# A transformer block with PEER: 160 tokens by gathers instead of 128, spread to the last steps, and their outputs made inside the main loop

## The chip, the cores and the metric

The kernel runs on one core of a Trainium2 chip. The metric is the time of one execution on the device, in microseconds (us). Engines: PE (TensorE, matmuls), DVE (VectorE), ACT (ScalarE), POOL (GpSimd), SP (SyncE, which here only issues DMAs).

## What is computed

One encoder layer for 512 tokens of width 1024: adaLN modulation, multi-head latent attention beside a gated MLP, a projection, and then PEER, 16,384 experts of a single neuron each. The part that the change touches is PEER and the final norm:

```python
def peer(h, w_q, keys, U, V):
    q = (ht @ w_q).reshape(T, 8, 2, 128)
    s1 = einsum('thd,hkd->thk', q[:, :, 0], keys[:, 0])     # 128 keys each
    s2 = einsum('thd,hkd->thk', q[:, :, 1], keys[:, 1])
    v1, i1 = top_k(s1, 16); v2, i2 = top_k(s2, 16)
    sc, ci = top_k(v1[..., :, None] + v2[..., None, :], 16) # of 256 sums
    idx = i1[ci // 16] * 128 + i2[ci % 16]                  # 8 x 16 experts a token
    gates = softmax(sc)
    a = einsum('chkd,cd->chk', U[idx], x)
    return einsum('chkd,chk->cd', V[idx], gelu(a) * gates)
x = x + gate2 * peer(h2);  out = rmsnorm(x) * g_final
```

So each token needs 128 rows of `U` and of `V` (16384 x 1024, float32).

## The kernel before

The 512 tokens are treated in two ways. `TD` = 384 tokens (blocks 0 to 2 of 128) are **dense**: all 16,384 experts are computed for them, 128 at a time, as matmuls, and a gate table `gd`, zero for experts that a token did not choose, picks out the right ones. Block 3 (`GB`) is **gathered**: for each of its tokens' 128 choices, an indirect DMA on POOL fetches 128 rows of `peer_u` (`gu`, `gather_u`, L871) and later of `peer_v` (`gv`, `gather_v`, L881), 512 KB at a time into one of four buffers (tag `g`); DVE multiplies a `gu` tile by the tokens and sums (L875), and adds a `gv` tile, weighted, to `accg` (L887).

Below, an expert e is a block of 128 neurons. Every float32 product is made of three matmuls of parts that PE takes (`mm3`, L80: high x high, high x low, low x high), so each operand is split first (`split_into`, L76: ACT copies the high part, DVE subtracts for the low part, `...h` and `...l`). For each expert, `a_mm` (L509) makes `pa`, 8 x 3 matmuls with the transposed tokens `h2T` moving (`TD` columns); ACT's gelu gives `a`; DVE multiplies `a` by the gate table (L938) and splits it into `w...h`, `w...l`; v is loaded and split (L935); then 3 token blocks x 2 halves x 3 = 18 matmuls add to the six accumulators `out0` to `out5` (512 columns each).

In time: 0 to 256 us, everything ahead of PEER; 256 to 455, queries, scores and routing of the dense blocks, with the first products of 20 experts between; 455 to 594, the gate table, in `NG = TD // UT` groups of eight tokens (`g_eq`, `g_gate`, `g_mm` L788, `g_evac`), with ten experts between; then the main loop of 128 steps. Step e makes `pa` of expert e + 30 (`AHEAD`; in steps 0 to 97) and `out` of expert e. The last four experts (`TAIL`, 124 to 127) are held and multiplied together at the end. After the loop each block's output is made: half by half a product with `gate2` out of `out...` (L979), an add of the residual `xr` (L980), ACT's squares, a root on POOL, the gain `gfin` (L985, L997) and two stores.

What goes between the steps is set by a planner: `fill` is a list of pieces of work with a cost, first the routing of block 3, then its 128 `gather_u`, then 128 `gather_v`. Each step has a `slack` (4.6 in steps with `pa`, 1.7 without, 0 in the last `END` = 8), and pieces are issued as the running sum of slack times `rate` (all costs over all slack) passes their costs. The pieces follow v's split in DVE's order. SP issues the loads of u, v, the gate table and `xr`, and half the stores, in the order of its queue.

Of the kernel before, what the change touches and what calls it, by code (L numbers as in the profile page):

```python
# [19 lines left out]
P = 128  # L20
# [9 lines left out]
TD = ND * P  # L30
# [6 lines left out]
END = 8  # L37
# [20 lines left out]
def tile_kernel(ctx: ExitStack, tc: tile.TileContext, a: dict, out: bass.AP):  # L58
# [442 lines left out]
    gtg = pp.tile([P, 1, PH, K], F32, name="gtg")  # L501
    jrep = pp.tile([P, K, K], BF16, name="jrep")
# [98 lines left out]
    def route_lookup(r, f, dst):  # L601
# [6 lines left out]
        nc.vector.tensor_tensor(oh, oh, r["rep"].pop(f), op=ALU.mult)  # L608
# [17 lines left out]
    with ExitStack() as qs:  # L626
# [8 lines left out]
        for b in range(NB):  # L635
            nc.vector.tensor_scalar_mul(xn[b], x2[b], r2[b])
        for j in range(KD):
            p = q_ps(f"trx2{j}")
            for b in range(ND):
                nc.tensor.transpose(p[:, b * P:(b + 1) * P], xn[b][:, j * P:(j + 1) * P], ident)  # L640
            t = W.tile([P, TD], F32, name=f"nt2_{j}", tag="qT", bufs=3)
            affine(j, t, p[:, :TD], s2, sh2)
            split_into(h2T[0][:, j, :TD], h2T[1][:, j, :TD], t)
# [9 lines left out]
        split_into(h2T[0][:, :, TD:], h2T[1][:, :, TD:], tg)  # L653
# [6 lines left out]
        nc.scalar.dma_start(h2gd, h2gt)  # L660
# [20 lines left out]
        def score(h):  # L681
            s_sb = R.tile([P, ND, 2, P], F32, name=f"s{h}", tag="s_sb", bufs=3)
            s_gb = R.tile([P, 2, P], F32, name=f"sg{h}", tag="s_gb", bufs=2)
            for f in range(2):
# [14 lines left out]
                nc.scalar.copy(s_sb[:, :, f, :], p[:, :TD].rearrange("p (b n) -> p b n", n=P))  # L699
                nc.scalar.copy(s_gb[:, f, :], p[:, TD:])  # L700
# [40 lines left out]
    flat = lambda t, b: t.rearrange("p b h k -> p b (h k)")[:, b, :]  # L741
    vp = pool(ctx, "vpool")
# [102 lines left out]
    def gb_open():  # L845
        st["stack"] = ExitStack()
        st["R"] = pool(st["stack"], "gbroute")
        st["sg"] = st["R"].tile([P, 2 * PH, P], F32, name="sgb")
        nc.sync.dma_start(st["sg"], sgd)
        st["r"] = route_tiles(st["R"], "g", 1, PH)  # L850
        st["sc"] = st["R"].tile([P, 1, PH, K], F32, name="scg")
        st["i"] = [st["R"].tile([P, 1, PH, K], F32, name=f"i{f}g") for f in range(2)]

    def gb_idx():
# [3 lines left out]
        st["gp"] = pool(ctx, "gpool")  # L858
        st["accg"] = st["gp"].tile([P, D], F32, name="accg")
        st["h2g"] = st["gp"].tile([P, D], F32, name="h2g")  # L860
        nc.sync.dma_start(st["h2g"], h2gd)
        st["actg"] = st["gp"].tile([P, NS], F32, name="actg")
        st["wg"] = st["gp"].tile([P, NS], F32, name="wg")

    def gather(src, s, name):
        g = st["gp"].tile([P, D], F32, name=name, tag="g", bufs=4)
        nc.gpsimd.indirect_dma_start(out=g, out_offset=None, in_=src,  # L867
                                     in_offset=bass.IndirectOffsetOnAxis(ap=idx[:, s:s + 1], axis=0))
        return g

    def gather_u(n):  # L871
        g = gather(a["peer_u"], n, f"gu{n}")
        actg, wg = st["actg"], st["wg"]
        scr = st["gp"].tile([P, D], BF16, name=f"scr{n}", tag="scr", bufs=1)
        nc.vector.scalar_tensor_tensor(scr, g, 1.0, st["h2g"], op0=ALU.mult, op1=ALU.mult,  # L875
                                       accum_out=actg[:, n:n + 1])
        if n == NS - 1:
            nc.scalar.activation(wg, actg, AF.Gelu)
# [10 lines left out]
    fill = []  # L889
    for h in range(PH):  # L890
        for f in range(2):
            fill.append((1.6, lambda h=h, f=f: route_keys(st["r"], 0, h, f, st["sg"][:, 2 * h + f, :])))
    fill.append((0.0, lambda: (route_tables(st["r"]), route_rep(st["r"], 0))))
    fill.append((1.2, lambda: route_cands(st["r"])))
    for h in range(PH):
        fill.append((1.3, lambda h=h: route_pick(st["r"], 0, h, st["sc"][:, 0, h, :])))
    fill.append((3.6, lambda: route_decode(st["r"])))
    fill.append((4.0, lambda: route_lookup(st["r"], 0, st["i"][0])))
    fill.append((0.0, lambda: route_rep(st["r"], 1)))
    fill.append((4.0, lambda: route_lookup(st["r"], 1, st["i"][1])))  # L900
    fill.append((1.2, lambda: route_gates(st["R"], st["sc"], gtg, PH)))
    fill.append((0.3, gb_idx))
# [10 lines left out]
    due = 0.0  # L913
    gb_open()
    for e in range(NE):
# [27 lines left out]
        if e < NE - TAIL or e == NE - 1:  # L943
            for b in range(ND):
                bs = slice(b * P, (b + 1) * P)
                for hf, (e_, wh, wl, vh, vl) in [(hf, h) for hf in range(2) for h in held]:
                    sl = slice(hf * 512, (hf + 1) * 512)
                    mm3(outs[2 * b + hf], (wh[:, bs], wl[:, bs]), (vh[:, sl], vl[:, sl]),
# [132 lines left out]
```

## Time and profile before

| | us |
|---|---|
| median of three runs | 1552.92 (1550.22 to 1554.04) |
| the profiled execution | 1551.62 |
| its span in the trace | 1549.8 |
| PE busy | 1485.2 (96%) |
| DVE busy | 1234.8 (80%) |
| ACT busy | 649.1 (42%) |
| POOL busy | 393.5 (25%) |
| DMA traffic | 380.72 MB, mean 246 GB/s |

The shares are over the whole span, and stages differ, so the rows below go stage by stage. Matmuls overlap each other: the printed duration of one is longer than the time from its start to the next one's, and only the pitch of starts says what one costs. A tile's number is its expert's or its gather's; where a view groups instructions, the number is left out.

### The profile page before, as it was taken

The numbers are of one execution on the slowest core, as the hardware profiler recorded it, in microseconds if no ns is written. First come the engines' busy times: TensorE is split into PE (matmuls) and PEld (weight loads), VectorE is DVE, ScalarE is ACT, GpSimd is POOL, SyncE is SP. The second block draws the span as 40 slices with busy tenths as digits, with TensorE's granted clock in tenths as the row PEclk, the third lists the DMA queues.
The fourth block names the chain that finished last, engine by engine and source line by source line (L and its number), as shares of the span: only waits on it lengthen the run. The fifth ranks groups of instructions, "written<-read, shape, count | busy, mean of one in ns | idle before, by whom it ended". The sixth has DMA issues, their size and how long they took to land.

```text
span 1549.8 us, 21464 instructions
## 1 busy us (share of the span) xinstructions
PE 1485.2 (96%) x7675; PEld 1311.7 (85%) x7675; DVE 1234.8 (80%) x2385; ACT 649.1 (42%) x1097; POOL 393.5 (25%) x335
## 2 busy tenths in 40 slices
PE   2898999999989999999999999999999999999997
PEld 1665687888979999999999999999999999998885
DVE  6937865569999997988878788788888788887774
ACT  2543434434459995443333333333333333333342
POOL 1212100000000000004444454444444444443210
PEclk9999999999989999999999999999999999999999
DMA  9626444331426778768999899898998899887872
GB/s 365 228 91 221 126 143 147 115 106 49 130 81 199 224 237 261 242 210 314 328 321 332 327 325 327 314 316 325 334 330 317 311 328 327 321 315 239 257 245 95
DMA packets 147228, 380.72 MB, mean 246 GB/s; under 512 B 11185, under 2 KB 59841, under 8 KB 146865
## 3 DMA queue, kind: packets, MB, share of 16 engines
q1 hardware_dynamic: 102896, 219.97, 40.6%
q0 software_dynamic: 42352, 153.62, 28.9%
q10 hardware_dynamic: 1872, 5.77, 1.0%
q8 instruction: 60, 0.98, 0.2%
q14 instruction: 48, 0.39, 0.1%
HBM read 349.16 MB, written 30.15 MB: 245 GB/s over the span
## 4 chain that ended last, share of the span: by engine, by line
PE 85%; DVE 8%; DMA 3%; issue 2%; ACT 1%; POOL 0%; SPq 0%; POOLq 0%; DVEq 0%; ACTq 0%
PE out L84 11%; PE out L83 11%; PE out L82 11%; PE pa L84 11%; PE pa L83 11%; PE pa L82 11%; PE gg L792 6%; DMA wada<-w_ada 2%; PE q L82 1%; PE q L83 1%; PE q L84 1%; DVE macc L149 1%; PE yo L83 1%; PE yo L84 1%; PE yo L82 1%
## 5 line engine op out<-in xcount | busy, mean ns | idle before, releaser
L867 POOL DMA_INDIRECT gu<-peer_u,idx x128 | 178.0, 1391 | 641.2 <-PE out L83 443.3
L867 POOL DMA_INDIRECT gv<-peer_v,idx x128 | 173.5, 1356 | 236.8 <-DVE accg L887 205.9
L887 DVE SCALAR_TENSOR_TENSOR accg<-gv,wg,accg 128x1024 f32<-128x1024 f32 x127 | 162.9, 1282 | 10.7 <-DMA gv<-peer_v,idx 8.5
L875 DVE SCALAR_TENSOR_TENSOR scr<-gu,h2g 128x1024 bf16<-128x1024 f32 x128 | 156.5, 1223 | 15.3 <-DMA gu<-peer_u,idx 12.9
L792 PE MATMUL gg<-o,o 128*128 128x128 f32 x768 | 96.1, 280 | 1.6 <-ACT o L786 1.6
L792 PEld LDWEIGHTS gg<-o,o 128*128 128x128 f32 x768 | 95.1, 196 | 1.9 <-ACT o L786 1.9
L938 DVE TENSOR_TENSOR a<-a,g 128x384 f32<-128x384 f32 x128 | 69.2, 551 | 4.7 <-ACT g L803 2.4
L786 ACT ACTIVATE o<-o1b,gT 128x128 f32<-128x128 bf16 x192 | 63.4, 404 | 13.2 <-PE gg L792 8.0
L518 ACT ACTIVATE a<-pa 128x384 f32<-128x384 f32 x128 | 61.5, 482 | 3.2 <-PE pa L84 3.1
L149 DVE SCALAR_TENSOR_TENSOR macc<-wada,csil,macc 128x1024 f32<-128x1024 f32 x40 | 51.3, 1282 | 10.5 <-DMA wada<-w_ada 10.1
L775 DVE TENSOR_TENSOR o<-iota_s,gT 128x1024 f32<-128x1024 f32 x48 | 58.7, 1222 | 0.6 <-PE gg L792 0.5
L779 DVE TENSOR_SCALAR o<-iota_s,gT 128x128 f32<-128x128 f32 x192 | 53.5, 345 | 0.0
L801 ACT COPY st<-gg 128x512 f32<-128x512 f32 x96 | 50.3, 578 | 0.0
L159 PE MATMUL mcol<-ident_s,macc 128*128 128x128 f32 x32 | 7.4, 390 | 26.7 <-DVE macc L146 22.8
L135 POOL DMA_DIRECT2D wada<-w_ada x32 | 17.1, 535 | 60.7 <-DVE macc L149 25.5
L159 PEld LDWEIGHTS mcol<-ident_s,macc 128*128 128x128 f32 x32 | 5.5, 201 | 28.5 <-DVE macc L146 18.3
L424 ACT ACTIVATE pe<-s,mx 128x512 f32<-128x512 f32 x16 | 11.0, 689 | 29.4 <-DVE mx L422 21.2
L773 DVE TENSOR_TENSOR o1b<-erep,gB 128x512 bf16<-128x512 bf16 x48 | 20.2, 422 | 1.1 <-ACT gB L756 1.1
L697 PE MATMUL sc<-keys_s,qT 128*128 128x128 f32 x128 | 18.0, 284 | 0.9 <-ACT qT L694 0.9
L697 PEld LDWEIGHTS sc<-keys_s,qT 128*128 128x128 f32 x128 | 15.5, 191 | 3.6 <-ACT qT L694 2.2
L531 DVE MAX8 v12d<-s 128x8 f32<-128x128 f32 x48 | 12.8, 285 | 6.9 <-ACT s L699 6.9
L418 PE MATMUL s<-kr,qr 64*128 64x512 f32 x32 | 18.0, 641 | 0.0
(2792 smaller groups left out, 4941.0 us busy)
## 6 DMA issues: line engine op xcount, KB each, us to landing
gd<-st SPq DMA_DIRECT2D x12, 1984.0 KB, 7.9
g<-gd SPq DMA_DIRECT2D x31, 768.0 KB, 8.5
wada<-w_ada POOLq DMA_DIRECT2D x32, 512.0 KB, 4.8
wada<-w_ada SPq DMA_DIRECT2D x16, 512.0 KB, 10.1
x<-x SPq DMA_DIRECT2D x4, 512.0 KB, 12.4
x<-x ACTq DMA_DIRECT2D x4, 512.0 KB, 4.1
x2d<-x ACTq DMA_DIRECT2D x4, 512.0 KB, 2.8
gu<-peer_u,idx POOLq DMA_INDIRECT x128, 7.0
```

Of the source, the lines that this page charges most:

```text
L82: nc.tensor.matmul(o, lhsT=lh, rhs=rh, start=first, stop=False)
L83: nc.tensor.matmul(o, lhsT=lh, rhs=rl, start=False, stop=False)
L84: nc.tensor.matmul(o, lhsT=ll, rhs=rh, start=False, stop=last)
L149: nc.vector.scalar_tensor_tensor(acc, w, csil[:, c:c + 1], acc, op0=ALU.mult, op1=ALU.add)
L518: nc.scalar.activation(t, p[:, :TD], AF.Gelu)
L775: nc.vector.tensor_tensor(o2s[n], iota.unsqueeze(1).to_broadcast([P, UT, P]), tT[:, 1, t0:t0 + UT].unsqueeze(2).to_broadcast([P, UT, P]), ...
L786: nc.scalar.activation(o1s[n][:, i, :], e[:, :, i], AF.Copy, scale=tT[:, 2, t0 + i:t0 + i + 1])
L792: nc.tensor.matmul(pgs[n][i // 4][:, i % 4 * P:(i % 4 + 1) * P], lhsT=o2[:, i, :], rhs=o1[:, i, :], start=True, stop=True)
L867: nc.gpsimd.indirect_dma_start(out=g, out_offset=None, in_=src, in_offset=bass.IndirectOffsetOnAxis(ap=idx[:, s:s + 1], axis=0))
L875: nc.vector.scalar_tensor_tensor(scr, g, 1.0, st["h2g"], op0=ALU.mult, op1=ALU.mult, accum_out=actg[:, n:n + 1])
L887: nc.vector.scalar_tensor_tensor(accg, g, wg[:, s:s + 1], accg, op0=ALU.mult, op1=ALU.add)
L938: nc.vector.tensor_tensor(wv3, wv3, gt[:, :, e % GE, :], op=ALU.mult)
```

## The change

Of the 384 dense tokens the last 32 (`XT`) are moved to gathers, so `TD` becomes 352 while the routing still covers `TR` = 384. For these 32 tokens the 128 choices are laid out as four quarters (`XQ`) of 32 choices (`XS`) over the 128 partitions: 32 `gather_u` and 32 `gather_v` more, with sums per quarter in `accx`, which a matmul with a 0/1 matrix `xsel` adds up (`px`, two halves). Their expert numbers and gates go through small DRAM tables (`xid`, `xgd`), their tokens through `h2gd`. The gate table has 44 groups instead of 48. `pa` is 352 columns wide. The third token block has 96 rows.

The planner's list becomes: one `gather_u` of the x tokens after each piece of routing, the rest of the routing, x's `gather_v`, block 3's gathers, and then the outputs of the x tokens and of block 3 as two pieces of cost 4.0. `END` is 3 instead of 8, and a late step's slack 2.0 instead of 1.7. The score tables of block 3 are loaded head by head, the copy `route_rep` is dropped in its lookups (the multiplication reads a broadcast), and the gathers' pool is opened at the loop's start. Cut to its core:

```diff
-TD = ND * P
+TR = ND * P
+XT = 32
+TD = TR - XT
+XQ = P // XT
+XS = NS // XQ
-END = 8
+END = 3
...
+        tx = XN.tile([P, KD, XT], F32, name="tx")
         for j in range(KD):
...
-            split_into(h2T[0][:, j, :TD], h2T[1][:, j, :TD], t)
+            split_into(h2T[0][:, j, :TR], h2T[1][:, j, :TR], t)
+            nc.vector.tensor_copy(tx[:, j, :], t[:, TD:])
...
+        h2xt = XN.tile([XT, D], F32, name="h2xt")
+        for i in range(2):
+            p = q_ps(f"h2xp{i}")
+            for j in range(4):
+                nc.tensor.transpose(p[:XT, j * P:(j + 1) * P], tx[:, 4 * i + j, :], ident)
+            nc.scalar.copy(h2xt[:, i * 512:(i + 1) * 512], p[:XT])
+        nc.scalar.dma_start(h2gd[P:], h2xt)
...
+    nc.vector.scalar_tensor_tensor(xi[xr_], flat(i1a, ND - 1)[xr_], 128.0, flat(i2a, ND - 1)[xr_],
+                                   op0=ALU.mult, op1=ALU.add)
+    nc.sync.dma_start(xid.rearrange("q t s -> t q s"), xi[xr_].rearrange("t (q s) -> t q s", q=XQ))
+    nc.sync.dma_start(xgd.rearrange("q t s -> t q s"), flat(gts, ND - 1)[xr_].rearrange("t (q s) -> t q s", q=XQ))
+    nc.sync.dma_start(idxx, xid.rearrange("q t s -> (q t) s"))
+    nc.sync.dma_start(gtx, xgd.rearrange("q t s -> (q t) s"))
...
+    def g_open(k, ns):
+        h2g = gp.tile([P, D], F32, name=f"h2g{k}", tag="h2g", bufs=1)
...
+        if b == "x":
+            p = psa.tile([P, 512], F32, name=f"px{hf}", tag="pa", bufs=2)
+            nc.tensor.matmul(p[:XT], lhsT=st["xsel"], rhs=gs_["x"]["acc"][:, halves[hf]], start=True, stop=True)
+            return p
...
+    for n in range(XS):
+        fill.append((1.3, lambda n=n: gather_u("x", idxx, gtx, n, XS)))
+        if n < len(route):
+            fill.append(route[n])
+    fill += route[XS:]
+    for n in range(XS):
+        fill.append((1.3, lambda n=n: gather_v("x", idxx, n)))
     for n in range(NS):
-        fill.append((1.3, lambda n=n: gather_u(n)))
+        fill.append((1.3, lambda n=n: gather_u("g", idx, flat(gtg, 0), n, NS)))
     for n in range(NS):
-        fill.append((1.3, lambda n=n: gather_v(n)))
-    slack = [4.6 if e + AHEAD < NE else 1.7 for e in range(NE)]
+        fill.append((1.3, lambda n=n: gather_v("g", idx, n)))
+    fill.append((0.3, out_open))
+    for b in ("x", GB):
+        fill.append((4.0, lambda b=b: output(b)))
+    slack = [4.6 if e + AHEAD < NE else 2.0 for e in range(NE)]
...
-                bs = slice(b * P, (b + 1) * P)
+                bs = slice(b * P, min((b + 1) * P, TD))
...
-    for b in (GB, 0, 1, 2):
+    for b in range(ND):
         o_load(b)
-        if b == GB:
-            o_sum(b, 0)
-            o_gain(b)
-            o_sum(b, 1)
-            o_root(b)
-            o_store(b)
```

What moves in the engines' orders, at three places. First DVE in the middle of the main loop, from one split of `w` to the next (`v...l` and `u...l` are splits, `accg` the sum over a gathered tile, `a` the gate product). Before:

```order
L78 TENSOR_TENSOR w74l_10964<-a74_8782,w74h_10963 128x384
L935 TENSOR_TENSOR v72l_10820<-v72r_10817,v72h_10819 128x1024
L887 SCALAR_TENSOR_TENSOR accg_6540<-gv33_10846,wg_6544,accg_6540 128x1024
L887 SCALAR_TENSOR_TENSOR accg_6540<-gv34_10849,wg_6544,accg_6540 128x1024
L887 SCALAR_TENSOR_TENSOR accg_6540<-gv35_10852,wg_6544,accg_6540 128x1024
L78 TENSOR_TENSOR u103l_10858<-u103r_10855,u103h_10857 128x1024
L938 TENSOR_TENSOR a101_10742<-a101_10742,g100_12688 128x384
L78 TENSOR_TENSOR w75l_11035<-a75_8858,w75h_11034 128x384
```

With the change:

```order
L82 TENSOR_TENSOR w78l_11361<-a78_9100,w78h_11360 128x352
L1063 TENSOR_TENSOR v76l_11211<-v76r_11208,v76h_11210 128x1024
L938 SCALAR_TENSOR_TENSOR accg_10737<-gvg21_11237,wgg_7844,accg_10737 128x1024
L938 SCALAR_TENSOR_TENSOR accg_10737<-gvg22_11240,wgg_7844,accg_10737 128x1024
L82 TENSOR_TENSOR u107l_11252<-u107r_11249,u107h_11251 128x1024
L938 SCALAR_TENSOR_TENSOR accg_10737<-gvg23_11243,wgg_7844,accg_10737 128x1024
L1066 TENSOR_TENSOR a105_11133<-a105_11133,g104_12971 128x352
L938 SCALAR_TENSOR_TENSOR accg_10737<-gvg24_11246,wgg_7844,accg_10737 128x1024
L82 TENSOR_TENSOR w79l_11432<-a79_9176,w79h_11431 128x352
```

Here four gathered tiles stand in a step instead of three, and the operations on `a` and `w` are 352 wide.

Second, DVE at the end of the loop, where the last experts' splits and the first output work stand. Before (`yf0` is the first product of block 0's output):

```order
L78 TENSOR_TENSOR w125l_13480<-a125_12443,w125h_13479 128x384
L935 TENSOR_TENSOR v123l_13433<-v123r_13430,v123h_13432 128x1024
L78 TENSOR_TENSOR w126l_13491<-a126_12511,w126h_13490 128x384
L935 TENSOR_TENSOR v124l_13464<-v124r_13461,v124h_13463 128x1024
L78 TENSOR_TENSOR w127l_13502<-a127_12584,w127h_13501 128x384
L935 TENSOR_TENSOR v125l_13475<-v125r_13472,v125h_13474 128x1024
L979 TENSOR_TENSOR yf0_13602<-out0_5451,gate2_84 128x512
```

With the change, from the x tokens' first product on (`yfx`, `ygx`, `ssfx`: the x tokens' output; `yf3`, `yg3`, `ssf3`: block 3's):

```order
L977 TENSOR_TENSOR yfx_13613<-px0_13616,gate2_84 32x512
L1063 TENSOR_TENSOR v124l_13670<-v124r_13667,v124h_13669 128x1024
L978 TENSOR_TENSOR yfx_13613<-yfx_13613,xrx_13611 32x512
L977 TENSOR_TENSOR yfx_13613<-px1_13622,gate2_84 32x512
L983 TENSOR_TENSOR ygx_13615<-yfx_13613,gfin_13549 32x512
L978 TENSOR_TENSOR yfx_13613<-yfx_13613,xrx_13611 32x512
L987 TENSOR_TENSOR ssfx_13614<-ssfx_13614 32x1
```

and right behind these rows:

```order
L977 TENSOR_TENSOR yf3_13680<-accg_10737,gate2_84 128x512
L118 TENSOR_SCALAR finx_ms_13628<-ssfx_13614 32x1
L977 TENSOR_TENSOR yf3_13680<-accg_10737,gate2_84 128x512
L994 SCALAR_TENSOR_TENSOR yfx_13613<-yfx_13613,finx_r_13630,gfin_13549 32x512
L978 TENSOR_TENSOR yf3_13680<-yf3_13680,xr3_13678 128x512 x2
L983 TENSOR_TENSOR yg3_13682<-yf3_13680,gfin_13549 128x512
L1063 TENSOR_TENSOR v125l_13702<-v125r_13699,v125h_13701 128x1024
L987 TENSOR_TENSOR ssf3_13681<-ssf3_13681 128x1
L82 TENSOR_TENSOR w127l_13729<-a127_12728,w127h_13728 128x352
L118 TENSOR_SCALAR fin3_ms_13691<-ssf3_13681 128x1
L994 SCALAR_TENSOR_TENSOR yf3_13680<-yf3_13680,fin3_r_13693,gfin_13549 128x512
L977 TENSOR_TENSOR yf0_13806<-out0_5381,gate2_84 128x512
```

The outputs of the x tokens and of block 3 now stand ahead of `v125l` and `w127l`; before, block 3's were done ahead of `w125l`. On PE the two matmuls of `px` stand ahead of the first one of expert 123.

Third, SP's queue at the end. Before:

```order
L971 DMA xr3_13579<-x2d_87 128x1024
L927 DMA v121r_13372<-peer_v 128x1024
L971 DMA xr0_13600<-x2d_87 128x1024
L927 DMA v122r_13401<-peer_v 128x1024
L927 DMA v123r_13430<-peer_v 128x1024
L1000 DMA out_0_dram<-yf3_13581 128x512
```

With the change:

```order
L1055 DMA v124r_13667<-peer_v 128x1024
L966 DMA xr1_13809<-x2d_87 128x1024
L966 DMA xr3_13678<-x2d_87 128x1024
L966 DMA xr2_13814<-x2d_87 96x1024
L997 DMA out_0_dram<-yfx_13613 32x512
L966 DMA xr0_13804<-x2d_87 128x1024
L997 DMA out_0_dram<-yf3_13680 128x512
```

Block 0's residual `xr0` was loaded before v122; now it comes after all expert loads and behind a store of the x tokens' output.

## Rows read from the trace of the kernel before

**Rows 1.** The page, chain that ended last, share by engine.
```profile
PE 85%; DVE 8%; DMA 3%; issue 2%; ACT 1%; POOL 0%; SPq 0%; POOLq 0%; DVEq 0%; ACTq 0%
```
**Rows 2.** Stretches: from:to, us, busy us (and instructions) per engine, PE clock, DMA share, GB/s.
```profile
345.00:452.00 107.00, 101.18 (x534) 90.72 (x532) 105.34 (x495) 47.88 (x64) 0.00 (x0) 1.00 0.32 104
455.00:594.00 139.00, 138.46 (x1053) 138.49 (x1054) 133.79 (x299) 125.40 (x323) 0.00 (x0) 0.98 0.67 205
594.00:720.00 126.00, 126.00 (x635) 114.81 (x634) 106.90 (x325) 52.60 (x71) 9.46 (x7) 1.00 0.72 246
1010.00:1300.00 290.00, 290.00 (x1456) 263.89 (x1455) 235.82 (x262) 101.05 (x141) 136.41 (x97) 1.00 0.90 323
```
**Rows 3.** Timeline of PE in the loop: start, us, instruction.
```profile
1189.69 0.34 PE L83 MATMUL pa<-h2T,u101h 128*128 128x384 f32 x1
...
1193.05 0.34 PE L84 MATMUL pa<-h2T,u101l 128*128 128x384 f32 x1
1193.23 0.39 PE L82 MATMUL out<-v71h,w71h 128*128 128x512 f32 x1
...
1197.12 0.40 PE L84 MATMUL out<-v71h,w71l 128*128 128x512 f32 x1
```
**Rows 4.** Timeline of DVE in the loop, with idle time before and what ended it.
```profile
1181.12 0.56 DVE L78 TENSOR_TENSOR w73l<-a,w73h 128x384 fp32r<-128x384 f32 x1 [0.75 <-ACT w73h L77]
1182.08 1.23 DVE L935 TENSOR_TENSOR v71l<-v71r,v71h 128x1024 fp32r<-128x1024 f32 x1 [0.40 <-ACT v71h L934]
1183.22 3.92 DVE L887 SCALAR_TENSOR_TENSOR accg<-gv,wg,accg 128x1024 f32<-128x1024 f32 x3
...
1189.50 0.56 DVE L78 TENSOR_TENSOR w74l<-a,w74h 128x384 fp32r<-128x384 f32 x1 [0.75 <-ACT w74h L77]
```
**Rows 5.** Chain in order of time: start, us, what; groups of the gate table.
```profile
463.14 1.78 PE gg L792 x16
...
590.93 1.78 PE gg L792 x16
```
**Rows 6.** The page, groups: busy us, mean ns | idle before, what ended it.
```profile
L887 DVE SCALAR_TENSOR_TENSOR accg<-gv,wg,accg 128x1024 f32<-128x1024 f32 x127 | 162.9, 1282 | 10.7 <-DMA gv<-peer_v,idx 8.5
L875 DVE SCALAR_TENSOR_TENSOR scr<-gu,h2g 128x1024 bf16<-128x1024 f32 x128 | 156.5, 1223 | 15.3 <-DMA gu<-peer_u,idx 12.9
```
**Rows 7.** Timeline of POOL in the same loop step.
```profile
1184.77 1.86 POOL L867 DMA_INDIRECT gv<-peer_v,idx  x1 [3.59 <-DVE accg L887]
```
**Rows 8.** The tile `gv`: time from issue to landing.
```profile
DMA to landing us min/median/max: 4.4/6.6/10.7
```
**Rows 9.** Timeline of DVE in steps without `pa`.
```profile
1419.66 0.56 DVE L78 TENSOR_TENSOR w102l<-a,w102h 128x384 fp32r<-128x384 f32 x1 [0.71 <-ACT w102h L77]
...
1423.74 0.56 DVE L78 TENSOR_TENSOR w103l<-a,w103h 128x384 fp32r<-128x384 f32 x1 [0.71 <-ACT w103h L77]
```
**Rows 10.** Timelines of PE (first row) and DVE at the end.
```profile
1517.06 0.39 PE L82 MATMUL out<-v123h,w123h 128*128 128x512 f32 x1
...
1526.17 0.69 DVE L979 TENSOR_TENSOR yf<-out,gate 128x512 f32<-128x512 f32 x1 [2.34 <-PE out L84]
...
1530.44 0.16 DVE L991 TENSOR_TENSOR ssf<-ssf 128x1 f32<-128x1 f32 x1 [0.79 <-ACT xr L981]
...
1541.63 0.75 DVE L997 SCALAR_TENSOR_TENSOR yf<-yf,fin_r,gfin 128x512 f32<-128x512 f32 x1 [0.72 <-POOL fin_r L114]
```
**Rows 11.** Chain in order of time: float32 matmuls of 512 columns.
```profile
81.83 1.72 PE qn L342 x4
```
**Rows 12.** DMA issues at the end: count, KB each, median us from issue to landing.
```profile
xr<-x2d SPq DMA_DIRECT2D x4, 512.0 KB, 4.0
out_dram<-yf SPq DMA_DIRECT2D x4, 256.0 KB, 2.3
```
**Rows 13.** DMA rate in slices of 5 us, from 1100 to 1300 us.
```profile
GB/s 273 348 297 339 412 336 313 202 366 269 413 368 343 256 252 310 310 412 398 271 341 301 216 350 330 346 321 296 358 228 388 377 347 305 358 203 314 380 388 301
```
**Rows 14.** The page, groups: the gate table's weight loads.
```profile
L792 PEld LDWEIGHTS gg<-o,o 128*128 128x128 f32 x768 | 95.1, 196 | 1.9 <-ACT o L786 1.9
```

More of the change, by code (lines that the diff above doesn't have):

```diff
@@ L857, in gb_idx, with gather @@
         st["stack"].close()
[L858 to L866, printed above, removed]
+        st["gp2"] = pool(ctx, "gpool2")
+    def gather(src, ix, s, name):
+        g = gp.tile([P, D], F32, name=name, tag="g", bufs=4)
@@ new lines, in g_open, with gather_u @@
+    def g_open(k, ns):
+        h2g = gp.tile([P, D], F32, name=f"h2g{k}", tag="h2g", bufs=1)
+        if k == "x":
+            for q in range(XQ):
+                nc.sync.dma_start(h2g[q * XT:(q + 1) * XT, :], h2gd[P:])
+        else:
+            nc.sync.dma_start(h2g, h2gd[:P])
+        gs_[k] = {"h2g": h2g,
+                  "act": gp.tile([P, ns], F32, name=f"act{k}"),
+                  "w": gp.tile([P, ns], F32, name=f"wg{k}")}
+    def gather_u(k, ix, gt_, n, ns):
+        if n == 0:
+            g_open(k, ns)
+        g = gather(a["peer_u"], ix, n, f"gu{k}{n}")
+        actg, wg = gs_[k]["act"], gs_[k]["w"]
+        scr = gp.tile([P, D], BF16, name=f"scr{k}{n}", tag="scr", bufs=1)
+        nc.vector.scalar_tensor_tensor(scr, g, 1.0, gs_[k]["h2g"], op0=ALU.mult, op1=ALU.mult,
@@ L887, in gather_v, with out_open @@
             nc.vector.scalar_tensor_tensor(accg, g, wg[:, s:s + 1], accg, op0=ALU.mult, op1=ALU.add)
-    fill = []
+    rows = {GB: (TR, T), "x": (TD, TR), 0: (0, P), 1: (P, 2 * P), 2: (2 * P, TD)}
+    halves = [slice(hf * 512, (hf + 1) * 512) for hf in range(2)]
+    outp, rs = {}, {}
+    def out_open():
+        st["gfin"] = gp.tile([P, D], F32, name="gfin", tag="g", bufs=4)
+        nc.sync.dma_start(st["gfin"], a["g_final"].partition_broadcast(P))
+        st["xsel"] = gp.tile([P, XT], F32, name="xsel")
+        nc.vector.reduce_sum(st["xsel"], ident.rearrange("p (q t) -> p t q", q=XQ), axis=AX.X)
@@ new lines, in o_store, with output @@
+    def o_store(b):
+        xr, y, ss, yg, n = outp[b]
+        r, (r0, r1) = rs[b][:, 0:1], rows[b]
+        nc.scalar.activation(yg, yg, AF.Copy, scale=r)
+        nc.vector.scalar_tensor_tensor(y[:, halves[1]], y[:, halves[1]], r, st["gfin"][:n, halves[1]],
+                                       op0=ALU.mult, op1=ALU.mult)
+        nc.scalar.dma_start(out[r0:r1, halves[0]], yg)
+        nc.sync.dma_start(out[r0:r1, halves[1]], y[:, halves[1]])
+    def output(b):
+        o_load(b)
+        o_sum(b, 0)
+        o_gain(b)
+        o_sum(b, 1)
+        o_root(b)
+        o_store(b)
@@ L897, in tile_kernel @@
[L897 to L902, printed above, removed]
+        route.append((1.3, lambda h=h: route_pick(st["r"], 0, h, st["sc"][:, 0, h, :])))
+    route.append((3.6, lambda: route_decode(st["r"])))
@@ L903, in tile_kernel @@
+    for f in range(2):
+        route.append((5.0, lambda f=f: route_lookup(st["r"], f, st["i"][f])))
+    route.append((1.2, lambda: route_gates(st["R"], st["sc"], gtg, PH)))
+    route.append((0.3, gb_idx))
+    fill = []
+    for n in range(XS):
[5 more added lines that the diff above has]
+        fill.append((1.3, lambda n=n: gather_v("x", idxx, n)))
     for n in range(NS):
-        fill.append((1.3, lambda n=n: gather_u(n)))
+        fill.append((1.3, lambda n=n: gather_u("g", idx, flat(gtg, 0), n, NS)))
@@ L913, in tile_kernel @@
     due = 0.0
+    gp = pool(ctx, "gpool")
     gb_open()
```

138 lines of the change are left out of this document (73 added, 65 removed).

## The prediction

> **What bounds the kernel now.** I read the chain of waits first: TensorE (PE) holds 85% of it, DVE 8% [rows 1]. Then busy time by stretch [rows 2]: in the main loop PE is busy 290.00 of 290.00 us with DVE at 235.82, so there a step lasts as long as its matmuls. Before the loop it differs: from 345 to 452 us DVE is busy 105.34 of 107.00, and from 455 to 594 us PE, DVE and ACT are all near full. The row to watch is the loop's: the change takes work from PE and gives DVE more, so I price both per step and see which is longer.
>
> PE's price comes from the pitch of starts, since the printed durations overlap. Twenty `pa` products of 384 columns start from 1189.69 to 1193.05: 3.36 / 19 = 0.177 us. Eighteen `out` products of 512 columns start from 1193.23 to 1197.12: 3.89 / 17 = 0.229 us [rows 3]. So 128 columns are worth 0.052 us, and 32 are worth 0.013. DVE's mid-loop step runs from the start of `w73l` to that of `w74l`: 1189.50 − 1181.12 = 8.38 us [rows 4], and 24 × 0.177 + 18 × 0.229 = 8.37 agrees.
>
> The sum below is made against the profiled execution's 1551.62 us (span 1549.8), 1.3 below the median of 1552.92. About 0.3%, 4.7 us, is what a measurement of this kernel can tell from no change.
>
> **The change part by part.**
>
> *Front, to 455 us.* Twenty experts' first products lose 480 × 0.013 = 6.2 us on PE, but DVE is the full engine there and its split of each expert is as wide as before. Added for it are eight small copies (each below the 0.56 us of an operation on 384 columns [rows 4]), then transposes and two copies on ACT. I take −1 and +1: 0, with ends −5 and +2. The four small DMAs added to SP stand between two expert loads that are fetched ahead; I cost them at nothing, and within the +2 if that cover is gone.
>
> *Gate table, 455 to 594.* A group of eight tokens recurs every (590.93 − 463.14) / 45 = 2.84 us [rows 5]. The table falls from 384 tokens to 352, 48 groups to 44, and PE, DVE and ACT all lose the same four: 48 × 2.84 = 136.3 becomes about 125.4. **−10.9**. The ten experts done between the groups are now spread over 44, which could leave DVE last: ends −8 and −11.4.
>
> *Loop, PE.* Only `pa` gets narrower: 24 × 0.013 = 0.31 us per step. The third output block has 96 rows instead of 128 but still streams 512 columns, so `out` keeps its price. A PE-bound step is 8.38 − 0.31 = 8.07.
>
> *Loop, DVE.* The planner's table gives the gathers per step. Before: 383.1 units of fill over 488.2 of slack, times 4.6 is 3.61 units or 2.78 gathers a step. After: 476.6 over 504.8, 4.34 units or 3.34 gathers a step, from about step 22 to step 97. Per step the other DVE work is v's split, u's split, the gate product and w's split: 1.23 each for the first two (one of them stands in the rows), about 0.56 each for the other two [rows 4]; less what overlaps it is 3.25, as the loop's total gives it (235.82 us over 290 / 8.38 = 34.6 steps is 6.81; less 2.78 × 1.28). At 352 columns it is 3.16. With 3.34 accumulations at 1.282 us or products at 1.223 us [rows 6] a step asks 7.44 or 7.24 us of DVE. Against 8.07 this leaves 0.63 to 0.83, so DVE still is not the longest by busy time, and what counts is how long it stands waiting for a gather.
>
> *Loop, waits for gathers.* Four buffers serve the gathers. POOL issues the next when DVE frees one: an accumulation of the three that start at 1183.22 ends near 1184.50, and POOL's gather starts at 1184.77 [rows 4, 7], 0.27 later. Landing takes 6.6 us in the median, 4.4 to 10.7 at the ends [rows 8], and use 1.28. That is 8.2 us of a buffer's cycle. Before, 97 gathers in 290 us [rows 2] grant 4 × 290 / 97 = 11.96 us: 3.8 to spare. After, 4 × 8.07 / 3.34 = 9.66: 1.5 to spare. Before, DVE waited 10.7 + 15.3 us over the 255 [rows 6], 0.10 each. With the spare cut to two fifths I take 0.24 each, an estimate in the same proportion, 0.80 a step, about the whole slack; lumps of it then reach PE. I take a step of 8.21 (ends 8.07, nothing reaching PE, and 8.6, where waits double again). 76 steps × (8.21 − 8.38) = **−12.9**; ends −23.6 and +17.
>
> *Steps 0 to 21.* Here the routing of the gathered block is filled in, and one x-gather with each piece. DVE was busy 106.90 of 126.00 [rows 2], 7.1 us a step; 0.73 more units add 0.6: 7.7 of 8.07. 22 × 0.31 is −6.9; the nearly full DVE and the first gathers (behind a load and a freed pool) give back an estimated 2: **−4.9**, ends −6.9 and +3.
>
> *Steps 98 to 123.* Only `out` remains, pitch 1423.74 − 1419.66 = 4.08 [rows 9], and the planner gives 1.46 gathers a step (1.03 before). DVE's step: 0.5 + 1.2 + 1.46 × 1.28 + 0.4 of waits for ACT = 4.0. Just fits: **+1**, ends 0 and +6.
>
> *End.* Two outputs, 32 rows and 128 rows, now sit in the last steps, behind which DVE has `v125l` and `w127l`, on which PE's last products wait. Count from T0, the start of step 123 on PE (1517.06 before); the first output's multiply of block 0 followed 9.1 us later [rows 10]. After: PE first runs the two selecting products, 4 records × 0.43 = 1.72 us [rows 11]. DVE takes the first at T0 + 0.9, then eleven half-width operations × 0.69, one split of 1.23, and waits as in the rows of before, 0.79 for ACT's squares and 0.72 for POOL's root [rows 10]: `v125l` ends near T0 + 12.7. PE, having run what it can (18 + 24 products × 0.229 + 1.72 = T0 + 11.3), stands 1.5 us. Block 0 is then whole at about T0 + 14.6 and its multiply starts at T0 + 15.1: **+6**, ends +2 and +9. On SP the load of block 0's `xr0` stands behind the store of the 32 rows, whose buffer it takes: multiplied at about T0 + 8.7, landed 2.3 later, and 4.0 for the load [rows 12] make T0 + 15.0, just ahead of its add at 15.8; if that store is late, the load is what is late next, and it sets the upper end. DVE's last run of output work (1526.17 to the product at 1541.63) starts 6 later and is as long as before; what the gathered block's output took here before was already under the loop's last matmuls.
>
> *Sum.* −10.9 + 0 − 4.9 − 12.9 + 1 + 6 = −21.7; 1551.6 − 21.7 = **1530 us**.
>
> **The rivals.**
>
> *All cover holds* (chance 0.09). No gather wait reaches PE and the end loses little: −11 + 0 − 7 − 24 and +3 to +7 for the last steps and the end is −39 to −35: 1513 to 1517. For it: DVE's busy time does fit. Against it: little spare is left in the four buffers.
>
> *The transfers' rate becomes the bound* (0.17). A step moves two expert blocks of 128 × 1024 × 4 bytes = 0.524 MB, 0.180 of gate table (128 × 352 × 4 bytes) and 3.34 gathers of 0.524: 2.98 MB. The loop ran 323 GB/s at a DMA share of 0.90 [rows 2], so 359 at full share: 8.30 us per step, 76 × −0.08 = −6, and 1537. Against it: single slices of 5 us reached 412 and 413 GB/s [rows 13]. The Trainium skill, page "DMA: Bandwidth & Descriptors", section "Where 436 GB/s comes from", says that between HBM and SBUF the HBM side binds, at about 358 GB/s for a core; by that figure a step would take 8.32 us and the kernel about 1538, and those slices of this trace speak against it as a hard limit for a core that is alone.
>
> *The four buffers' round trip becomes the bound* (0.14; the slower one). If the denser gathers land later, a step becomes 3.34 × (0.27 + L + 1.28) / 4, whatever PE needs. The rest of the sum is −8.8, so it stops being a gain at a step of 8.50, a mean landing of 8.6 us; at L = 9 the step is 8.81 and the kernel 1551.6 − 8.8 + 33 = 1576. For it: single landings of 10.7, and a DMA share that would go from 0.90 to near 1. Against it: the median of 6.6 at that 0.90.
>
> *Narrower products are no cheaper* (0.05). If loading the 128 × 128 weights set the pitch, 352 columns would take as long as 384. The weight load's record is 196 ns [rows 14], longer than the 0.177 of the pitch. Against it: sixteen such loads with 128 columns take 1.78 us, 0.111 each [rows 5], so a load of 196 ns overlaps its neighbours. Then the loop gains nothing and the table only the four groups' own products, 4 × 1.78 = 7: 1551.6 − 7 + 1 + 6, about 1552.
>
> **How the numbers follow.** The forecast has 0.55, spread from about 1522 to 1542. The range leaves out most of the buffers' rival above 1554 and half of the best case below 1514: 1514 to 1554. Faster by over 0.3%: nearly all of the forecast (0.52), the best case (0.09) and most of the rate's rival (0.14): 0.75. Within: some of each, and narrower products that are no cheaper: 0.12. Slower: mainly the buffers' rival, 0.13.
>
> **What would show it.** Gate table about 125 us long; `pa` pitch 0.164; steps 22 to 97 at 8.1 to 8.3 with some PE idle on `w…l` or `u…l` and more DVE idle on gathers; last steps still 4.1; about 15 us from T0 to block 0's multiply. The forecast is wrong if steps stay at 8.38 or above (landing beyond 8 us), if `pa` keeps 0.177, or if the end costs over 10 us.

## The result and the profile after

The changed kernel takes 1541.93 us (median of four runs, 1539.0 to 1542.88) where the kernel before took 1552.12 in the same comparison: a ratio of 0.9934, interval 0.992 to 0.9947. That is 10.2 us faster. The direction was right and the time lies in the range, but the gain is less than half of the 22 us that were forecast. The profiled execution took 1542.68 us, span 1540.8.

The page of the changed kernel, busy time and the chain that ended last, against [rows 1]:

```profile
PE 1452.5 (94%) x7623; PEld 1240.4 (81%) x7623; DVE 1279.7 (83%) x2476; ACT 638.9 (41%) x1078; POOL 455.7 (30%) x400
...
PE 41%; DMA 24%; DVE 16%; issue 10%; ACT 4%; POOL 4%; SPq 0%; POOLq 0%; DVEq 0%; ACTq 0%
DMA gug<-peer_u,idx 10%; DMA gvg<-peer_v,idx 8%; PE out L86 4%; PE out L87 4%; PE out L88 4%; PE pa L88 3%; PE pa L87 3%; PE pa L86 3%; POOL gvg L901 2%; DMA wada<-w_ada 2%; PE gg L822 2%; ACT o L816 2%; POOL gug L901 2%; PE q L87 1%; PE q L88 1%
```

PE's share of the chain fell from 85% to 41%, and the landings of gathers, which did not show among its lines before, hold 18%. The loop's stretch and the gathers' groups, against [rows 2] and [rows 6]:

```profile
1010.00:1300.00 290.00, 283.85 (x1474) 246.96 (x1474) 252.99 (x321) 103.51 (x143) 149.38 (x117) 1.00 0.97 362
```

```profile
L924 DVE SCALAR_TENSOR_TENSOR scrg<-gug,h2gg 128x1024 bf16<-128x1024 f32 x128 | 156.4, 1222 | 45.7 <-DMA gug<-peer_u,idx 44.6
L938 DVE SCALAR_TENSOR_TENSOR accg<-gvg,wgg,accg 128x1024 f32<-128x1024 f32 x127 | 163.0, 1284 | 28.8 <-DMA gvg<-peer_v,idx 27.6
```

PE no longer fills the loop: 6 us of 290 are idle. DVE's wait for the gathers of block 3 grew from 26.0 to 74.5 us. The landing of a `gv` tile, against [rows 8], rose from 6.6 to 7.4 us in the median:

```profile
DMA to landing us min/median/max: 4.9/7.4/10.1
```

By stretch, from the starts of the first instructions named (timelines of both kernels), in us:

| stretch | before | after | difference | forecast |
|---|---|---|---|---|
| start to first gate product `gg` | 455.5 | 461.2 | +5.7 | 0 |
| first to last `gg` product | 136.9 | 127.8 | −9.1 | −10.9 |
| to the first `out` of expert 22 | 190.5 | 187.3 | −3.2 | −4.9 |
| to `out` of expert 98 | 632.1 | 620.3 | −11.8 | −12.9 |
| to `out` of expert 122 | 97.9 | 105.9 | **+8.0** | +1 |
| to block 0's first multiply | 13.2 | 18.1 | +4.9 | +6 |
| to the end of the span | 23.6 | 20.2 | −3.4 | 0 |

The differences add up to −8.9, which is what separates the two profiled executions. Two lines carry the miss: the front and the steps without first products. The large loop term came out near its forecast; whether for the reason given is what the experiments ask first.

### The profile page after: what moved, and what is told of

Its sections match the earlier page's. It is cut to its first block, busy times and chain, and to the rows that moved or that the text cites. A ratio compares the mean times of both kernels' runs of the same rounds, so it can differ in the third digit from the quotient of the medians.

```text
span 1540.8 us, 21600 instructions
## 1 busy us (share of the span) xinstructions
PE 1452.5 (94%) x7623; PEld 1240.4 (81%) x7623; DVE 1279.7 (83%) x2476; ACT 638.9 (41%) x1078; POOL 455.7 (30%) x400
## 4 chain that ended last, share of the span: by engine, by line
PE 41%; DMA 24%; DVE 16%; issue 10%; ACT 4%; POOL 4%; SPq 0%; POOLq 0%; DVEq 0%; ACTq 0%
DMA gug<-peer_u,idx 10%; DMA gvg<-peer_v,idx 8%; PE out L86 4%; PE out L87 4%; PE out L88 4%; PE pa L88 3%; PE pa L87 3%; PE pa L86 3%; POOL gvg L901 2%; DMA wada<-w_ada 2%; PE gg L822 2%; ACT o L816 2%; POOL gug L901 2%; PE q L87 1%; PE q L88 1%
## 5 line engine op out<-in xcount | busy, mean ns | idle before, releaser
L901 POOL DMA_INDIRECT gug<-peer_u,idx x128 | 169.8, 1327 | 147.5 <-DVE scrg L924 123.2
L901 POOL DMA_INDIRECT gvg<-peer_v,idx x128 | 160.2, 1251 | 170.1 <-DVE accg L938 145.7
L924 DVE SCALAR_TENSOR_TENSOR scrg<-gug,h2gg 128x1024 bf16<-128x1024 f32 x128 | 156.4, 1222 | 45.7 <-DMA gug<-peer_u,idx 44.6
L938 DVE SCALAR_TENSOR_TENSOR accg<-gvg,wgg,accg 128x1024 f32<-128x1024 f32 x127 | 163.0, 1284 | 28.8 <-DMA gvg<-peer_v,idx 27.6
L901 POOL DMA_INDIRECT gux<-peer_u,idxx x32 | 41.4, 1293 | 439.5 <-DMA u34r<-u_t 342.1
L1066 DVE TENSOR_TENSOR a<-a,g 128x352 f32<-128x352 f32 x128 | 64.7, 516 | 3.5 <-ACT g L833 2.2
L816 ACT ACTIVATE o<-o1b,gT 128x128 f32<-128x128 bf16 x176 | 58.1, 404 | 12.9 <-PE gg L822 7.4
L526 ACT ACTIVATE a<-pa 128x352 f32<-128x352 f32 x128 | 58.3, 456 | 1.5 <-PE pa L88 1.4
L901 POOL DMA_INDIRECT gvx<-peer_v,idxx x32 | 41.3, 1292 | 55.8 <-DVE accx L938 32.1
L938 DVE SCALAR_TENSOR_TENSOR accx<-gvx,wgx,accx 128x1024 f32<-128x1024 f32 x31 | 39.8, 1284 | 8.7 <-DMA gvx<-peer_v,idxx 8.5
L924 DVE SCALAR_TENSOR_TENSOR scrx<-gux,h2gx 128x1024 bf16<-128x1024 f32 x32 | 38.7, 1210 | 4.9 <-DMA gux<-peer_u,idxx 4.9
L165 PEld LDWEIGHTS mcol<-ident_s,macc 128*128 128x128 f32 x32 | 5.2, 194 | 29.1 <-DVE macc L152 18.1
```

The costliest lines, as they stand in the source:

```text
L526: nc.scalar.activation(t, p[:, :TD], AF.Gelu)
L816: nc.scalar.activation(o1s[n][:, i, :], e[:, :, i], AF.Copy, scale=tT[:, 2, t0 + i:t0 + i + 1])
L924: nc.vector.scalar_tensor_tensor(scr, g, 1.0, gs_[k]["h2g"], op0=ALU.mult, op1=ALU.mult, accum_out=actg[:, n:n + 1])
L938: nc.vector.scalar_tensor_tensor(accg, g, wg[:, s:s + 1], accg, op0=ALU.mult, op1=ALU.add)
L1066: nc.vector.tensor_tensor(wv3, wv3, gt[:, :, e % GE, :], op=ALU.mult)
```

## The experiments

Unless named otherwise each is the changed kernel with one edit. Ratios are against the kernel before, run beside it.

**Buffers: six and five in the changed kernel, six and three in the kernel before.** The two extra buffers take memory that is free once routing is done:

```diff
     def gather(src, ix, s, name):
-        g = gp.tile([P, D], F32, name=name, tag="g", bufs=4)
+        if "gp2" in st and s % NGB >= 4:
+            g = st["gp2"].tile([P, D], F32, name=name, tag="g2", bufs=NGB - 4)
+        else:
+            g = gp.tile([P, D], F32, name=name, tag="g", bufs=4)
```

Six, `NGB` = 6:

> The changed kernel with a ring of six gather buffers instead of four once the routing is done. Theory, round trip of the buffers: with six the gathers are asked for earlier, DVE's waits for them in steps 22 to 97 (now 45.7 + 28.8 us) fall to a few us, the step falls from 8.30 to 8.07 to 8.12, and the time by 13 to 17 us, to about 1527. Rival, rate of the transfers: the loop already moves 362 GB/s at a DMA share of 0.97; the landing only gets longer, the step stays at 8.25 to 8.30 and the time at 1538 to 1542.

Measured: 1520.46 us, ratio 0.979 (0.9774 to 0.9807), 21 us less than with four. The loop's stretch and two groups of this kernel:

```profile
1010.00:1300.00 290.00, 290.00 (x1531) 257.14 (x1530) 266.07 (x328) 104.28 (x147) 167.50 (x121) 1.00 0.99 376
```

```profile
L942 DVE SCALAR_TENSOR_TENSOR accg<-gvg,wgg,accg 128x1024 f32<-128x1024 f32 x127 | 163.7, 1289 | 1.6 <-DMA gvg<-peer_v,idx 0.2
...
L928 DVE SCALAR_TENSOR_TENSOR scrg<-gug,h2gg 128x1024 bf16<-128x1024 f32 x128 | 156.2, 1220 | 4.2 <-DMA gug<-peer_u,idx 2.8
```

PE is full again, DVE waits 5.8 us instead of 74.5, and the rate is 376 GB/s, above the 362 at which the rival saw a bound. From the first product of expert 60 to that of expert 110 it takes 398.3 us, 7.97 a step, against 8.18 with four; from `out` of expert 22 to that of 98 it takes 601.6 against 620.3. Five buffers:

> The changed kernel with five gather buffers. Theory, round trip: five buffers grant 5 x 7.97 / 3.34 = 11.9 us a cycle, as the kernel before had (12.0), so PE's idle time in steps 22 to 97 is gone as with six: step 7.97 to 8.0, time 1520 to 1523. Rival, the gathers need a long queue to reach the 381 GB/s: five give half of the win, 1529 to 1534.

Measured: 1522.78, ratio 0.9815 (0.9798 to 0.9831), the same step of 7.97 and the same 601.6 us. One buffer more is enough for the loop. Next the kernel before, `bufs` of tag `g` set to 6 and to 3:

> The kernel before with six gather buffers. Theory: at 2.78 gathers a step four buffers grant 12 us for a cycle of 8.7, so DVE's waits shrink but PE stands nowhere for them: the step stays 8.37, the time within 2 us of before. Rival, more gathers in flight help of themselves: 1545 or less.

Measured: 1551.0, ratio 0.9996 (0.9987 to 1.0006), as the theory had it.

> The kernel before with three gather buffers, which grant 3 x 8.37 / 2.78 = 9.0 us for a cycle of 8.7, as little to spare as the changed kernel has (9.6 for 9.0). Theory: waits for gathers reach PE here too, without any of the change's other parts: the step rises from 8.37 to 8.6 or 8.9 and the time by 15 to 40 us. Rival, buffers are not what sets the wait: the time within 4 us of before.

Measured: 1580.45, ratio 1.0177 (1.0156 to 1.0198), 28 us slower; the stretch from `out` of expert 22 to that of 98 grew from 632.1 to 663.6. Its chain and two groups:

```profile
PE 49%; DMA 24%; issue 10%; DVE 10%; POOL 4%; ACT 1%; DVEq 0%; SPq 0%; POOLq 0%; ACTq 0%
...
L875 DVE SCALAR_TENSOR_TENSOR scr<-gu,h2g 128x1024 bf16<-128x1024 f32 x128 | 156.5, 1223 | 103.6 <-DMA gu<-peer_u,idx 102.4
...
L887 DVE SCALAR_TENSOR_TENSOR accg<-gv,wg,accg 128x1024 f32<-128x1024 f32 x127 | 162.7, 1281 | 79.0 <-DMA gv<-peer_v,idx 78.1
```

The chain looks like that of the changed kernel, with nothing of the change in it. Buffers against the density of gathers are the cause of PE's waits in the loop.

**Narrower products alone**, in the kernel before (`TN` = 352; ACT fills the other 32 columns with zeros):

```diff
-        mm3(p[:, :TD], (hl[0][:, c, :], hl[1][:, c, :]), (h2T[0][:, c, :TD], h2T[1][:, c, :TD]),
+        mm3(p[:, :TN], (hl[0][:, c, :], hl[1][:, c, :]), (h2T[0][:, c, :TN], h2T[1][:, c, :TN]),
...
-        nc.scalar.activation(t, p[:, :TD], AF.Gelu)
+        nc.scalar.activation(t[:, :TN], p[:, :TN], AF.Gelu)
+        nc.scalar.copy(t[:, TN:], zer)
```

> The kernel before with one thing of the change: the first products are 352 columns wide, so the experts' part of 32 tokens is left out (zeros stand in for it); gathers, gate table and end are as before. Theory: the delay ahead of the gate table comes from the narrower products alone, through the order in which PE's queue then has experts 8 and 9 among the queries; the first gate product then starts near 461 us as in the changed kernel, not at 455.5. Rival: the delay comes from the added copies and transposes; it then starts at 455.5 or a little earlier. Both: a main-loop step falls from 8.37 to 8.07 us, because the gathers are as sparse as before, 98 steps give about -29, so about 1529 (theory) or 1523 (rival).

Measured: 1516.32, ratio 0.9769 (0.9752 to 0.9785). The first gate product starts at 460.75, so the delay is there without the copies and transposes that the change adds: that rival falls. This kernel's own small ACT copy of zeros for each expert was not tried by itself. The time is below both figures because the step is 7.93, not 8.07: `pa` has a pitch of 0.160 us at 352 columns, as two rows of the changed kernel show, (1232.77 − 1229.56) / 20:

```profile
1229.56 0.33 PE L86 MATMUL pa<-h2T,u108h 128*128 128x352 f32 x1
...
1232.77 0.32 PE L88 MATMUL pa<-h2T,u108l 128*128 128x352 f32 x1
```

**Front order.** What PE waits for in the front of the changed kernel, from its timeline:

```profile
382.80 0.32 PE L87 MATMUL pa<-h2T,u9h 128*128 128x352 f32 x1
387.05 0.66 PE L88 MATMUL pa<-h2T,u8l 128*128 128x352 f32 x1 [3.93 <-DVE u8l L82]
...
389.37 0.77 PE L86 MATMUL q<-h2T,wq13h 128*128 128x512 f32 x1
```

In its queue two products of expert 9 and two of expert 8 stand ahead of the queries of `wq13`. DVE has not yet split expert 8, PE stands 3.93 us, and the queries behind, which the routing needs, are late. In the kernel before, two products of expert 8 stood there and nothing of expert 9, and PE had no such wait. The edit holds each front expert behind the one before it (`mm3` returns its last matmul for that):

```diff
+        with ExitStack() as ia:
+            if c == 0 and last_pa and e < 20:
+                ia.enter_context(tc.issue_after(last_pa[0].ins))
+            last_pa[:] = [mm3(...)]
```

> The changed kernel; on PE each front expert's first product is held behind the last product of the expert before it, which puts the queries' products back ahead of expert 9. Theory, order in PE's queue: the first gate product starts at 455 to 457 us instead of 461.2 and the time falls by 4 to 6 us, to about 1536.5. Rival, added copies and transposes: it stays at 460 to 461 and the time within 2 us of 1542.

Measured: 1542.21, ratio 0.9924 (0.9903 to 0.9945): no gain in time. The last query product starts at 404.7 (before 405.1, changed 410.8) and the first gate product at 458.4: the order accounts for all of the delay at the queries and half of that at the gate table. The other traces agree, though the front differs between executions: the first gate product starts at 453.2 to 455.5 in the three kernels with the old front, at 460.7 to 465.0 in the six with the changed one, and at 457.5 to 458.5 in the four with this edit. The other half comes later: DVE waits 2.94 us for expert 18's high part, which ACT copies behind a wait of 4.84 for PE. It was not tried further. By expert 22 this kernel was 3.7 us ahead of the changed one, by expert 98 it was 3.1 behind: in this execution the loop with four buffers took the win away. So it was repeated with six:

> Six buffers and the front order. With four buffers the 6 us that the front order won were gone by step 98. Theory: there the gathers' round trip set the loop's end, and with six buffers, where PE sets the step at 7.97, the win stays: 5 to 6 us less than six buffers alone, about 1515. Rival: the win is lost in any case, to something that starts at a fixed time, as the loads: 1519 to 1522.

Measured: 1517.25, ratio 0.9768 (0.9752 to 0.9785), 3.2 below six buffers alone, with intervals that overlap. In the trace the first gate product is 6.1 us earlier (some of that because the six buffers' trace has a late front, 464.6), and 7.3 of lead at expert 22 is still 7.3 at expert 98. The theory's mechanism holds in the trace: what the front wins is kept. In time it was forecast at 5 to 6, and 3.2 is not clear of noise.

**Late steps.** The chain of the changed kernel at their start (in order of time: start, us, what):

```profile
1395.08 5.77 DMA gvg<-peer_v,idx
...
1407.00 1.23 DVE v100l L1063
...
1408.24 7.21 DMA v102r<-peer_v
```

A late gather holds v's splits in DVE's order; v102 is loaded only when v100 is split, and lands 7.21 us later. What PE lost lies earlier. It stood for expert 98's split, which DVE reached behind the loop's gathers:

```profile
1399.60 0.50 PE L87 MATMUL out<-v98l,w98h 128*128 128x512 f32 x1 [2.61 <-DVE v98l L1063]
```

From the first product of expert 98 to that of 99 it takes 8.61 us, in the next four steps 4.1 to 4.3. In the 8.61 are 2.61 of waiting, and right behind them, from 1400 to 1404 us, a granted clock of 0.57, near the lower of TensorE's two levels (1.2 and 2.4 GHz). The step of expert 102 takes 4.29, so the load that the chain names cost PE little. The edit opens five raw tiles for v instead of two:

```diff
-        if e < NE - 3:
+        if e < NE - 3 and (e + AHEAD < NE or e % 5 < 2):
             vraw = vp.tile([P, D], F32, name=f"v{e}r", tag="vr", bufs=2)
```

> The changed kernel; in the steps without first products the raw v tiles go round five buffers (two of their own and the three that the u tiles no longer need) instead of two. Theory, the loads of v are late because only two buffers are open and the gathers beside them stretch a landing from 4.4 to 5.9 us: steps 98 to 122 return from 4.4 to 4.08 us and the time falls by 5 to 8 us, to about 1535. Rival, DVE's own work (1.46 gathers a step) sets these steps: no change, 1540 to 1543.

Measured: 1540.7, ratio 0.9928 (0.9908 to 0.9949): not distinguishable from the changed kernel. In its trace the stretch from expert 98 to 122 fell from 105.9 to 101.9, but this execution came into the loop later and lost the rest there. What the tiles are worth is not shown: the front order's kernel, also with four gather buffers and with two raw tiles, has 103.3 there, and in both PE waits for one split alone, that of expert 98 (2.06 and 1.92 us). Six gather buffers alone bring the stretch to 101.0, and expert 98's products to 4.10: once DVE is not behind at step 98, most of the loss is gone.

**Outputs earlier**, six buffers and `END = 8`:

> Six buffers, and END = 8 instead of 3, so the fill, with the two outputs, is done by step 119. Theory: the outputs ahead of the last splits cost 4.9 us at the end (from expert 122's first product to the first output's multiply 18.1 us, before 13.2); with END = 8 that stretch returns to 13 to 14 us and the time falls by 3 to 5 us, to about 1516.5. Rival: the same 9 us of output work stands ahead of the split of v120 instead, and PE stands there as long: the sum from expert 110 to the multiply stays within 1 us of the 69.0 of six buffers, time 1519 to 1522.

Measured: 1516.43, ratio 0.9774 (0.9756 to 0.9792). From expert 122's first product (1479.37) to the multiply below it takes 13.5 us, where six buffers alone have 18.1:

```profile
1492.88 0.69 DVE L981 TENSOR_TENSOR yf<-out,gate 128x512 f32<-128x512 f32 x1 [2.36 <-PE out L89]
```

Part of these 4.6 us is only moved: with `END = 8` the two selecting products of PE stand ahead of expert 122, in a step of 6.11. From expert 110 to the multiply it takes 65.6 against 69.0, so 3.4 are won and the rival (within 1) falls. In time the gain of 4.0 has overlapping intervals.

**First x gathers four pieces of routing later**, six buffers:

> Six buffers, and the x gathers start four pieces of routing later than in the changed kernel. Theory: from the first products of expert 30 to those of expert 35 the changed kernel takes 46.5 us (five steps of 7.97 are 39.9) because DVE stands in its order before the first gathered tile, which waits for a pool's memory and a 10 us landing; started later they find data, this stretch falls to 40 to 42 us and the time from 1520.5 (six buffers) to about 1515. Rival: the wait only moves to where the gathers now start, since the first landing is as long: the sum from expert 30 to 45 stays at 126.7 us within 2, time 1519 to 1522.

Measured: 1519.11, ratio 0.9778 (0.9762 to 0.9795). From expert 30 to 45 it takes 126.1 us (six buffers 126.7). The first stretch did fall, from 47.0 to 42.4, and experts 40 to 45 lost it again: the rival holds.

**The edits together**, and then with a late step's slack of 1.2:

> Six buffers, front order, later x gathers, END = 8 and the ring of five raw v tiles together. If each is worth what its theory says and they add, 1520.5 - 5.5 - 5 - 4 - 3 = 1503; by the rivals 1518 to 1522.

> The five edits together, and a late step's slack 1.2 instead of 2.0, so about 0.93 gathers a late step instead of 1.48 and about 3.65 instead of 3.4 in the main steps. Theory, DVE's own work is what the late steps lose by now: from the first `out` of expert 98 to that of 122 it takes 101.8 us with the five edits, 97.9 before; it returns to 98 to 99, and the main step stays at 7.97 because DVE then asks 7.85 of it; time 3 us lower, about 1510. Rival, main steps now have too much: DVE becomes the bound there, the step rises to 8.1 or more, and the time is 1515 to 1522.

Measured: 1513.7, ratio 0.9755 (0.9738 to 0.9771), and 1512.99, ratio 0.9747 (0.973 to 0.9763). The edits do not add up to 1503: the profiled execution came near it (1507.78), the others were at 1512.7 to 1515.8. Fewer late gathers gained nothing in the late steps (102.6 against 101.8), so DVE was not their bound; and 3.65 gathers in a main step did not make it one there, at 7.97, as the theory said. For the late steps and the time, theory and rival both miss. What both kernels have there beyond the 97.9 of before is mostly PE's own: 1.9 us of selecting products, which `END = 8` puts into this stretch, and 1.6 of a slower pitch (last section). Either kernel beats the changed one by 28 us or more and the kernel before by 38.

## Why the prediction was half right

**Gate table** (−10.9, measured −9.1). Right in kind; the groups' pitch rose a little, and the chain now passes through DVE's expert splits there, which was the bound at −8.

**Loop, steps 22 to 97** (−12.9, measured −11.8). That the sum came out is luck: two errors offset each other. A PE-bound step is 7.97, not 8.07, because the first products lose 0.017 us for 32 columns, not 0.013: I had taken the slope between 384 and 512 columns of two different products. Without waits the stretch falls by 632.1 − 601.6 = 30.5 us, where I had 23.6. And the waits took back 620.3 − 601.6 = 18.7, or 0.25 a step, where I had 0.14, a share of DVE's waiting that I took without a working. DVE's waiting itself was close: 74.5 / 255 = 0.29 us a gather, forecast 0.24. The mechanism named, gathers whose four buffers have too little to spare, is shown by experiments on both kernels.

**The rivals.** The rate as a bound falls: 376 GB/s with six buffers, 388 in the kernel with fewer late gathers:

```profile
1010.00:1300.00 290.00, 290.00 (x1532) 257.18 (x1531) 273.49 (x320) 104.19 (x147) 175.65 (x128) 1.00 1.00 388
```

The Trainium skill, page "DMA: Bandwidth & Descriptors", section "Where 436 GB/s comes from", puts the HBM limit of a core at about 358 GB/s; these runs of one core go beyond it over 290 us, and the measurement decides. The rival of the buffers' round trip is what happened in kind, but its formula is not what decides: at the landing of 7.4 it gives 3.34 × 8.95 / 4 = 7.47, below PE's 7.97, and PE still waited. A gather that has landed also waits its turn in DVE's order, behind splits. By subtraction, a cycle of 4 × 8.16 / 3.34 = 9.77 us less 8.95 leaves 0.8 for that. The same sum for three buffers in the kernel before, with its step of 8.78 and a landing of 6.1, is 9.47 − 7.65 = 1.8. That narrower products are no cheaper is refuted by their pitch.

**Front** (0, measured +5.7). This step failed. I priced instructions on the engine that was full and took the order as given; the shorter products let the scheduler write another order into PE's queue, and PE, in order, stood behind a split that DVE, the full engine, had not made. It was there to be read: the built kernel's order has those rows ahead of `wq13`. The stretches with a stall also have a lower granted clock, between TensorE's two levels of 1.2 and 2.4 GHz: 0.83 from 385 to 395 us, where the kernel before had 1.00. Ahead of the gate table PE waits for the routing in both kernels: from 450 to 460 us it was busy 6.00 us before and 2.44 after, at a clock of 0.55 and 0.58, and then the changed kernel stays low for longer. Before, from 460 us, and then the changed kernel:

```profile
460.00:470.00 10.00, 10.00 (x76) 10.00 (x76) 9.51 (x21) 8.16 (x22) 0.00 (x0) 0.93 0.05 7
```

```profile
460.00:470.00 10.00, 8.76 (x58) 8.79 (x58) 9.70 (x24) 7.66 (x23) 0.00 (x0) 0.73 0.02 3
```

**Steps 0 to 21** (−4.9, measured −3.2). The cheaper step is worth 22 × 0.40 = 8.8; the first gathers cost 5.6 of it, not 2. Starting them later only moves that.

**Steps 98 to 123** (+1, measured +8.0). The other step that failed. I added up DVE's work and found it just fits, as if DVE came to step 98 on time and v were always there. DVE came late from the loop's gathers: the first three steps take 16.9 us, 12.2 before and 12.4 with six buffers, which is 4.5 of the 8.0. Of the 3.1 that are left with six buffers (3.9 and 4.2 in two more kernels with six) about 1.6 is PE's own pitch (below); the rest is in single steps in which PE waits for a split. What v's loads have in that was not separated.

**End** (+6, measured +4.9). Right: PE ran the two selecting products first, block 0's multiply came 13.9 us after them (forecast 15.1), and the last splits stood behind the outputs:

```profile
1506.73 1.90 PE L956 MATMUL px<-accx,xsel 128*32 128x512 f32 x4
```

```profile
1517.17 1.21 DVE L1063 TENSOR_TENSOR v125l<-v125r,v125h 128x1024 fp32r<-128x1024 f32 x1
...
1520.60 0.69 DVE L977 TENSOR_TENSOR yf<-out,gate 128x512 f32<-128x512 f32 x1 [0.15 <-PE out L88]
```

None of the prediction's signs of being wrong appeared: they watched the loop's step, `pa`'s pitch and the end, not the two terms that failed. The last stretch gave 3.4 us that the sum did not have, so without that the miss would be larger. What I could have concluded from my own sum: with 1.5 us to spare in a buffer's cycle, late landings reach DVE, and whoever is next in DVE's order, in the loop and behind it.

## What to carry to other kernels

Where transfers go round a ring of buffers, compare the cycle that the ring grants (buffers × step / transfers per step) with landing plus use: 3.8 us to spare cost nothing here, 1.5 by the landing of before (0.6 by the 7.4 then measured: 4 × 7.97 / 3.34 − 8.95) cost 19 us over the loop, and one more buffer gave it back. Look for memory that a finished stage has freed before giving up on a deeper ring. After any change of an instruction's length, read the new order of the in-order queues ahead of the full engine's waits: there a shorter instruction can cost time. Where a chain names a load, look whether the bound engine waited for it.

## What was not expected of the hardware

`pa` falls from 0.177 to 0.160 us between 384 and 352 columns, a little more than the columns' share. The `out` products, with as many columns as before, became slower where only they run: from expert 98 to 122 the mean pitch is 0.227 us before and with narrower products alone, 0.230 to 0.231 in all kernels whose third block has 96 rows, also with fewer gathers beside them. The 96 rows were not tried by themselves; over 24 steps of 18 this is 1.6 us of the late steps.

From the start of DVE's last product to the end of the span it takes 8.2 us in the kernel before, in its variants and with narrower products alone, and 4.8 in the changed kernel and all its variants. In the trace POOL's closing drain takes 8.0 us in the one and 4.6 in the other. That gave 3.4 us that nothing in the change explains; it was not followed up.
